# A fixed order for the first product of a one-core decoder trunk, with x in five loads

## Chip, core and metric

One of the eight cores of one Trainium2 chip runs the whole program, batch 1, 256 tokens, float32. The time is the device time of one execution in microseconds (us). The engines named below are PE (TensorE, the matrix engine, with PEld for its weight loads), DVE (VectorE), ACT (ScalarE), POOL (GpSimd) and SP (SyncE, which here only issues DMAs). "ACTq" and "SPq" are the instruction queues of those engines, on which DMA issues and waits stand in line with everything else.

## What is computed

One layer of a macaron block, then a final norm. All weights are float32, D_MODEL is 2048, D_FF is 5632:

```python
def swiglu(h, w_gate, w_up, w_down):
    return (jax.nn.silu(h @ w_gate) * (h @ w_up)) @ w_down

x = x + 0.5 * swiglu(rmsnorm(x, ffn1_norm), ffn1_w_gate, ffn1_w_up, ffn1_w_down)
x = x + hybrid_mixer(rmsnorm(x, mix_norm), w_in, conv_w, pool_w, pool_scale, w_out)
x = x + 0.5 * swiglu(rmsnorm(x, ffn2_norm), ffn2_w_gate, ffn2_w_up, ffn2_w_down)
return rmsnorm(x, final_norm)
```

The change touches the very first product, `x @ ffn1_w_gate` for the first 512 of its 5632 columns, and the way to it.

## The kernel before

**Tiles.** x lies in four tiles `xr[n]`, each 128 tokens x 2 x 512 channels. A product has the tokens as output rows, so the left operand is x transposed, 128 channels (one k of 16) by 256 tokens. The full float32 precision comes from three products per k: every operand is split into a high part that the matrix engine takes (`wh`, `xh`) and the remainder (`wl`, `xl`), and `gemm` (L142) adds hi x wh, lo x wh and hi x wl. With two blocks of 128 tokens that is 6 matmuls per k and 96 for one block of 512 columns (`ag` for the gate, `au` for up, `ad` for down).

**Weights.** `gemm` loads four k at a time into a tile `wt` (L174, on SP's queue, four buffers); ACT copies it to `wh` (L180) and DVE forms `wl` (L181). A `wt` buffer is free for the next load once `wl` is made.

**The first product.** Here the left operand does not exist yet. `first_block` loads x tile by tile, and `gained(..., at_once=True)` (L245) lets PE transpose a tile of 512 channels into one PSUM tile `tp` (8 transposes, L230), then per 128 channels ACT writes `xh` with the norm's gain as a scale (L252) and DVE writes `xl` (L253). The gains come from `prm`, which is itself a transposed load of `rows` (L80, `pp` L87, L88). The weights of this product are cut into 1, 1, 2, 4, 4 and 4 k. While nothing has arrived PE transposes an identity 14 times (`spin`, L101). ACT's queue also issues the DMA of `pw` (L334, used only in the mixer) and the four later parameter rows (L80).

**What sets the order.** A scheduler that simulates the program places the instructions of each engine, so those of different k, and of `ag` and `au`, stand interleaved. Both readers of `tp` carry waits: within one `tp` tile the `xh` of a block waits for the `xl` of the block before it. All else (`ffn` L276, `mixer` L329) runs on the same `gemm`.

Of the kernel before, what the change touches and what calls it, by code (L numbers as in the profile page):

```python
# [1 line left out]

# [6 lines left out]
F32 = mybir.dt.float32  # L9
F32R = mybir.dt.float32r  # L10
# [14 lines left out]
def hybrid_trunk(ctx, tc, x, ffn1_norm, ffn1_w_gate, ffn1_w_up, ffn1_w_down, mix_norm, w_in,  # L25
# [34 lines left out]
    def load_x(n):  # L60
        nc.sync.dma_start(out=xr[n], in_=xv[:, :, n * NB:(n + 1) * NB])


    small, col = [], {}
# [7 lines left out]
    NP = sum(r.shape[0] for r in small)  # L72
    prm = pool.tile([P, NP], F32, name="prm")

    def load_params(which, at):
        n = sum(r.shape[0] for r in which)
        rows = pool.tile([n, P], F32, name="rows", tag="rows", bufs=1)
        r0 = 0
        for v in which:
            nc.scalar.dma_start(out=rows[r0:r0 + v.shape[0], :], in_=v)  # L80
            r0 += v.shape[0]
        return rows, at, n

# [3 lines left out]
        nc.tensor.transpose(pp[:, :n], rows, ident[:n, :n])  # L87
        nc.vector.tensor_copy(out=prm[:, at:at + n], in_=pp[:, :n])  # L88

    first_params = load_params(small[:1], 0)  # L90
    load_x(0)
    ident = pool.tile([P, P], F32, name="ident")
    make_identity(nc, ident)
    mhalf = pool.tile([P, T], F32, name="mhalf")
# [4 lines left out]
    spin = tp_tile("spin")
    for i in range(14):  # L100
        nc.tensor.transpose(spin[:, :P], ident, ident)  # L101
    place_params(first_params)

# [34 lines left out]
    later = []  # L140

    def gemm(lhs, w, n0, ks, name, cuts=None, before=None, by_tile=None):  # L142
# [25 lines left out]
        cuts = cuts or [CH] * (nk // CH)  # L168
        for ci, m in enumerate(cuts):
            kk = ks[c0:c0 + m]  # L170
            if before:
                before(kk[0])
            wt = stat.tile([P, CH, NB], F32, name="wt", tag="wt", bufs=4)
            nc.sync.dma_start(  # L174
                out=wt[:, :m],
                in_=w[kk[0] * P:(kk[-1] + 1) * P, n0:n0 + NB].rearrange("(k p) n -> p k n", p=P))
            wh = stat.tile([P, CH, NB], F32R, name="wh", tag="wh", bufs=3)
            wl = stat.tile([P, CH, NB], F32R, name="wl", tag="wl", bufs=3)
            with nullcontext() if before else tc.high_priority():
                high[0] = nc.scalar.activation(out=wh[:, :m], in_=wt[:, :m], func=AF.Copy)  # L180
                nc.vector.tensor_sub(out=wl[:, :m], in0=wt[:, :m], in1=wh[:, :m].bitcast(F32))  # L181
            if by_tile and ci >= len(cuts) - 3:
                held.append((c0, kk, wh, wl))
            else:
                for i, k in enumerate(kk):
                    for t in range(T):
                        products(t, c0 + i, [k], wh[:, i:i + 1], wl[:, i:i + 1])
            c0 += m
            step()
        if by_tile:  # L190
            for t in range(T):
                for h in held:
                    products(t, *h)
                by_tile(t, acc_of[t])
        return acc
# [46 lines left out]
                                    in_=sv[a * Q:(a + 1) * Q, :, :, j, :])  # L242
        return dst

    def gained(n, c0, at_once=False):  # L245

        tp = transposed(xr[n]) if at_once else turned(xr[n], work([P, 4, S], "xt"))
        hi = stat.tile([P, 4, S], F32R, name="xh", tag="xh", bufs=4)
        lo = stat.tile([P, 4, S], F32R, name="xl", tag="xl", bufs=4)
        for i in range(4):  # L250
            g = prm[:, c0 + 4 * n + i:c0 + 4 * n + i + 1]
            nc.scalar.activation(out=hi[:, i, :], in_=tp[:, i, :], func=AF.Copy, scale=g)  # L252
            nc.vector.scalar_tensor_tensor(out=lo[:, i, :], in0=tp[:, i, :], scalar=g,  # L253
                                           in1=hi[:, i, :].bitcast(F32), op0=ALU.mult,
                                           op1=ALU.subtract)
        return hi, lo

# [4 lines left out]
    def block_of(tiles):  # L262
        def block(k):
            while k // 4 not in tiles:
                step()
            hi, lo = tiles[k // 4]
            return hi[:, k % 4, :], lo[:, k % 4, :]
        return block

    def residual(acc, n, factor, ts=range(T)):  # L270
# [2 lines left out]
                                           in1=xr[n][:, t, :], op0=ALU.mult, op1=ALU.add)  # L273


    def ffn(xt, rs, wg, wu, wd, after, cuts=None, before=None, last_tile=None):  # L276

        ht = {}  # L280

        def hidden(j, **first):
            ag = gemm(block_of(xt), wg, j * NB, range(KD), "ag", **first)
# [24 lines left out]
            later.append(turn)  # L308

        for j0 in range(0, FB, 6):  # L310
            js = range(j0, min(j0 + 6, FB))
            for j in js:
                hidden(j, **(dict(cuts=cuts, before=before) if j == 0 else {}))
            ks = range(4 * js[0], 4 * js[-1] + 4)
            done = js[-1] == FB - 1
            for n in range(DN):
                if done and n == DN - 1 and last_tile:
                    def tile_done(t, acc, n=n):
                        residual(acc, n, 0.5, [t])
                        last_tile(t)  # L320
                    gemm(block_of(ht), wd, n * NB, ks, "ad", by_tile=tile_done)
                    continue
                acc = gemm(block_of(ht), wd, n * NB, ks, "ad")
                residual(acc, n, 0.5)
                if done:
                    after(n)


    def mixer(l, xt, rs_of, after):  # L329
# [198 lines left out]
    def first_block(k):
        if k % 4 == 0:
            n = k // 4  # L530
            if n:
                load_x(n)
            xt[n] = gained(n, col["ffn1", 0], at_once=True)
# [88 lines left out]
```

## Time and profile before

| | us |
|---|---|
| median of 3 runs (1793.63 to 1793.72) | 1793.68 |
| the profiled execution | 1793.22 |
| its span, first to last instruction | 1791.1 |
| PE busy in it | 1776.9 (99%) |
| DVE busy | 1144.3 (64%) |
| ACT busy | 748.6 (42%) |

PE's busy share says that it nearly always has a matmul in flight, not that each is as fast as it can be; a row with 0.39 us duration stands 0.23 us after the row before it, since matmuls overlap. Only gaps on PE, and changes of its clock, can make this program longer or shorter.

### The profile page before, as it was taken

The page shows a single profiled execution, that of the slowest core. Times are in us where ns is not written, and L with a number is a line of the kernel's source. Part 1 is how long each engine was busy: PE and PEld are TensorE (multiplying, and loading weights), DVE is VectorE, ACT ScalarE, POOL GpSimd, SP SyncE. Part 2 cuts the span into 40 slices and gives each one's busy share as a digit, 9 for nine tenths or more (in the row PEclk, how much of TensorE's full clock was granted, in tenths as well). Part 3 has the DMA queues.
Part 4 walks back from the last instruction along what each step waited for, and adds up shares of the span by engine and source line. Part 5 has one row for each costly group of instructions (what it writes and reads, how often), then busy time and mean ns, then how long its engine had stood idle before and what let it go on. Part 6 is the DMA issues. An engine that isn't in the chain of part 4 may idle for free.

```text
span 1791.1 us, 19137 instructions
## 1 busy us (share of the span) xinstructions
PE 1776.9 (99%) x7928; PEld 1464.4 (82%) x7928; DVE 1144.3 (64%) x1260; ACT 748.6 (42%) x598; POOL 5.5 (0%) x19
## 2 busy tenths in 40 slices
PE   8999999999999999999999999999999999999998
PEld 7888888888888888887778888888888888888886
DVE  5766666444666687768767896666664446666653
ACT  6434433333344344545544455443443334433342
POOL 0000000000000000000000000000000000000000
PEclk9999999999999999999999999999999999999999
DMA  8655555555555555554545555555556555555652
GB/s 289 211 189 196 199 192 188 190 201 196 188 190 198 198 181 195 197 199 146 188 141 188 167 207 190 188 188 194 198 197 209 189 189 196 199 191 188 218 197 78
DMA packets 172262, 342.32 MB, mean 191 GB/s; under 512 B 5456, under 2 KB 6032, under 8 KB 172176
## 3 DMA queue, kind: packets, MB, share of 16 engines
q1 hardware_dynamic: 171232, 339.76, 56.2%
q10 hardware_dynamic: 944, 1.34, 0.3%
q8 instruction: 62, 1.02, 0.2%
q14 instruction: 24, 0.20, 0.0%
HBM read 338.98 MB, written 2.10 MB: 190 GB/s over the span
## 4 chain that ended last, share of the span: by engine, by line
PE 98%; DVE 1%; DMA 0%; ACT 0%; issue 0%; ACTq 0%; POOLq 0%
PE au L164 9%; PE ad L166 9%; PE au L165 9%; PE ad L164 9%; PE au L166 9%; PE ad L165 9%; PE ag L166 9%; PE ag L164 9%; PE ag L165 9%; PE az L164 4%; PE az L166 4%; PE az L165 4%; PE ao L166 1%; PE ao L165 1%; PE ao L164 1%; DVE wl L181 0%
## 5 line engine op out<-in xcount | busy, mean ns | idle before, releaser
L181 DVE TENSOR_TENSOR wl<-wt,wh 128x2048 fp32r<-128x2048 f32 (+1 forms) x322 | 732.8, 2277 | 543.4 <-ACT wh L180 541.4
L180 ACT ACTIVATE wh<-wt 128x2048 fp32r<-128x2048 f32 (+1 forms) x322 | 613.6, 1905 | 867.0 <-PE au L165 281.3
L164 PE MATMUL ag<-wh,xh 128*128 128x512 f32 x704 | 274.8, 390 | 2.1 <-ACT xh L252 2.1
L165 PE MATMUL ag<-wh,xl 128*128 128x512 f32 x704 | 274.6, 390 | 0.3 <-DVE xl L253 0.3
L166 PE MATMUL ag<-wl,xh 128*128 128x512 f32 x704 | 274.5, 390 | 0.2 <-DVE wl L181 0.2
L164 PE MATMUL au<-wh,xh 128*128 128x512 f32 x704 | 274.0, 389 | 0.0
L165 PE MATMUL au<-wh,xl 128*128 128x512 f32 x704 | 273.9, 389 | 0.0
L166 PE MATMUL au<-wl,xh 128*128 128x512 f32 x704 | 273.9, 389 | 0.0
L165 PE MATMUL ad<-wh,hl 128*128 128x512 f32 x704 | 273.9, 389 | 0.0
L164 PE MATMUL ad<-wh,hh 128*128 128x512 f32 x704 | 273.9, 389 | 0.0
L166 PE MATMUL ad<-wl,hh 128*128 128x512 f32 x704 | 273.7, 389 | 0.0
L241 DVE STREAM_TRANSPOSE ht<-h 32x256 f32<-32x256 f32 x352 | 153.5, 436 | 5.6
L164 PEld LDWEIGHTS ag<-wh,xh 128*128 128x128 f32 x704 | 132.4, 188 | 29.7 <-ACT xh L252 2.4
L166 PEld LDWEIGHTS ag<-wl,xh 128*128 128x128 f32 x704 | 132.5, 188 | 28.0 <-DVE wl L181 0.6
L165 PEld LDWEIGHTS ag<-wh,xl 128*128 128x128 f32 x704 | 132.4, 188 | 28.1 <-DVE xl L253 0.8
L165 PEld LDWEIGHTS ad<-wh,hl 128*128 128x128 f32 x704 | 132.2, 188 | 27.5
L164 PEld LDWEIGHTS au<-wh,xh 128*128 128x128 f32 x704 | 132.2, 188 | 27.5
L166 PEld LDWEIGHTS au<-wl,xh 128*128 128x128 f32 x704 | 132.2, 188 | 27.4
L166 PEld LDWEIGHTS ad<-wl,hh 128*128 128x128 f32 x704 | 132.2, 188 | 27.4
L165 PEld LDWEIGHTS au<-wh,xl 128*128 128x128 f32 x704 | 132.2, 188 | 27.3
L164 PEld LDWEIGHTS ad<-wh,hh 128*128 128x128 f32 x704 | 132.2, 188 | 27.3
L164 PE MATMUL az<-wh,xh 128*128 128x512 f32 x320 | 126.8, 396 | 0.0
(116 smaller groups left out, 1142.1 us busy)
## 6 DMA issues: line engine op xcount, KB each, us to landing
wt<-in_ffn_w_up_dram SPq DMA_DIRECT2D x88, 1024.0 KB, 5.1
wt<-in_ffn_w_down_dram SPq DMA_DIRECT2D x88, 1024.0 KB, 5.1
wt<-in_ffn_w_gate_dram SPq DMA_DIRECT2D x87, 1024.0 KB, 5.1
wt<-in_w_in_dram SPq DMA_DIRECT2D x40, 1024.0 KB, 5.0
wt<-in_w_out_dram SPq DMA_DIRECT2D x16, 1024.0 KB, 5.1
x<-in_x_dram SPq DMA_DIRECT2D x4, 512.0 KB, 10.3
out_dram<-xg SPq DMA_DIRECT2D x8, 256.0 KB, 3.1
gf<-in_final_norm_dram ACTq DMA_DIRECT2D x2, 512.0 KB, 4.7
```

What stands on the lines that cost most here:

```text
L164: nc.tensor.matmul(acc_of[t][:, t, :], lhsT=hi[:, ts], rhs=wh[:, i, :], start=first, stop=False)
L165: nc.tensor.matmul(acc_of[t][:, t, :], lhsT=lo[:, ts], rhs=wh[:, i, :], start=False, stop=False)
L166: nc.tensor.matmul(acc_of[t][:, t, :], lhsT=hi[:, ts], rhs=wl[:, i, :], start=False, stop=last)
L180: high[0] = nc.scalar.activation(out=wh[:, :m], in_=wt[:, :m], func=AF.Copy)
L181: nc.vector.tensor_sub(out=wl[:, :m], in0=wt[:, :m], in1=wh[:, :m].bitcast(F32))
L241: nc.vector.transpose(out=dv[j * Q:(j + 1) * Q, :, :, a, :], in_=sv[a * Q:(a + 1) * Q, :, :, j, :])
```

## The change

The first product gets a function of its own, `opening`, whose instructions stay in the order in which they are written (`manual_schedule`). x is loaded in five pieces: the first tile in two halves, then three whole tiles, between weight loads of 1, 1, 2, 2, 2, 2, 2, 2 and 2 k. Each 128 channels of `xh` and `xl` have a tile of their own. For a k the six matmuls run hi, hi, lo, lo, hi, hi over both token blocks. Of the identity transposes 12 stand ahead of the gains and 5 behind the first transposes of x. The later parameter rows go from ACT's queue to POOL's, and `pw` goes to SP's queue behind the last load of the first feed-forward. The second feed-forward no longer repeats eight sums of squares (`add_stats(ss0, n)`), which it did since a non-empty `first` was passed to it.

```diff
-    first_params = load_params(small[:1], 0)
-    load_x(0)
+    first_params = load_params(small[:1], 0, nc.scalar)
...
+    def opening(xt, c0, w, name):
+        acc = psum.tile([P, T, NB], F32, name=name, tag="acc", bufs=2)
+        pieces = {}
+        def prepare(n, blocks):
+            if n not in pieces:
+                pieces[n] = tp_tile("tp").rearrange("p (k s) -> p k s", k=4)
+                xt[n] = split_tiles()
+            for i in blocks:
+                for t in range(T):
+                    nc.tensor.transpose(pieces[n][:, i, t * P:(t + 1) * P],
+                                        xr[n][:, t, i * P:(i + 1) * P], ident)
+            return n, blocks
+        def ready(n, blocks):
+            gain_split(pieces[n], xt[n], n, c0, blocks)
+        def products(k, wh, wl, i):
+            hi, lo = (v[k % 4] for v in xt[k // 4])
+            for a, b, at in ((hi, wh, 0), (lo, wh, 1), (hi, wl, 2)):
+                for t in range(T):
+                    nc.tensor.matmul(acc[:, t, :], lhsT=a[:, t * P:(t + 1) * P], rhs=b[:, i, :],
+                                     start=k == 0 and at == 0, stop=k == KD - 1 and at == 2)
+        H = NB // 2
+        load_x(0, 0, H)
+        ws = {0: load_w(w, 0, [0])}
+        load_x(0, H, NB)
+        ws[1] = load_w(w, 0, [1])
+        ws[2] = load_w(w, 0, [2, 3])
+        load_x(1)
+        ws[4] = load_w(w, 0, [4, 5])
+        spin(12)
+        place_params(first_params)
+        prepare(0, [0, 1])
+        spin(5)
+        ready(0, [0])
+        h0 = split_w(ws[0], 1)
+        ready(0, [1])
+        h1 = split_w(ws[1], 1)
+        products(0, *h0, 0)
+        prepare(0, [2, 3])
+        ready(0, [2, 3])
+        h2 = split_w(ws[2], 2)
+        products(1, *h1, 0)
+        products(2, *h2, 0)
+        for k in range(3, KD):
+            if k % 4 == 3 and k + 1 < KD:
+                n = (k + 1) // 4
+                ws[k + 3] = load_w(w, 0, [k + 3, k + 4])
+                if n + 1 < DN:
+                    load_x(n + 1)
+                    ws[k + 5] = load_w(w, 0, [k + 5, k + 6])
+                prepare(n, range(4))
+                ready(n, range(4))
+            if k % 2:
+                products(k, *h2, 1)
+                if k + 1 < KD:
+                    h2 = split_w(ws[k + 1], 2)
+            else:
+                products(k, *h2, 0)
+        return acc
...
-            if first:
+            ag = first(wg) if first else gemm(block_of(xt), wg, j * NB, range(KD), "ag")
...
-        nc.scalar.dma_start(out=pw, in_=pool_w[l].rearrange("g c d -> c g d"))
+        with tc.issue_after(loaded[0].ins):
+            nc.sync.dma_start(out=pw, in_=pool_w[l].rearrange("g c d -> c g d"))
...
-        hi = stat.tile([P, 4, S], F32R, name="xh", tag="xh", bufs=4)
-        lo = stat.tile([P, 4, S], F32R, name="xl", tag="xl", bufs=4)
+        return ([stat.tile([P, S], F32R, name="xh", tag="xh", bufs=16) for i in range(4)],
+                [stat.tile([P, S], F32R, name="xl", tag="xl", bufs=16) for i in range(4)])
...
+    def begin(wg):
+        with tc.manual_schedule():
+            return opening(xt, col["ffn1", 0], wg, "ag")
...
-            more = load_params(small[1:], small[0].shape[0])
+            more = load_params(small[1:], small[0].shape[0], nc.gpsimd)
```

`load_w` and `split_w` are the load and the two split instructions of `gemm`; `gain_split` is the loop of `gained`.

ACT's queue from the first weights on, before. `waits` names the semaphores of an instruction: DMAHW a transfer, DVE, PE and Activation an engine. `tp_107` holds channels 0 to 511 of x, `tp_169` the next 512.

```order
L334 DMA pw_4654<-in_pool_w_dram 128x4x128
L180 ACTIVATE wh_128<-wt_126 128x512 [waits DMAHW2_49]
L80 DMA rows_460<-in_mix_norm_dram 16x128 [waits DMAHW1_49,DMAHW0_49,PE_49]
L80 DMA rows_460<-in_ffn2_norm_dram 16x128 [waits DMAHW3_49]
L252 ACTIVATE xh_116<-tp_107,prm_68 128x256 [waits DVE_49,PE_49]
L180 ACTIVATE wh_140<-wt_138 128x512 [waits DMAHW4_49]
L80 DMA rows_460<-in_conv_w_dram 12x128 [waits DMAHW5_49]
L180 ACTIVATE wh_152<-wt_150 128x1024
```

ACT's queue from the first weights (behind the first `xh`) to those of k = 4 to 7, in the change; `tp_117` is the first tile of x, `tp_183` the second.

```order
L153 ACTIVATE wh_138<-wt_91 128x512 [waits DMAHW2_49]
L329 ACTIVATE xh_119<-tp_117,prm_68 128x256 [waits DVE_49]
L153 ACTIVATE wh_144<-wt_94 128x512 [waits DMAHW4_49]
L329 ACTIVATE xh_120<-tp_117,prm_68 128x256 [waits DVE_49,PE_49]
L329 ACTIVATE xh_121<-tp_117,prm_68 128x256 [waits DVE_49]
L153 ACTIVATE wh_162<-wt_96 128x1024 [waits DMAHW5_49]
L329 ACTIVATE xh_184<-tp_183,prm_68 128x256 [waits PE_49]
L329 ACTIVATE xh_185<-tp_183,prm_68 128x256 [waits DVE_49]
L329 ACTIVATE xh_186<-tp_183,prm_68 128x256 [waits DVE_49]
L329 ACTIVATE xh_187<-tp_183,prm_68 128x256 [waits DVE_49]
L153 ACTIVATE wh_214<-wt_99 128x1024 [waits DMAHW7_49,Activation_49]
L153 ACTIVATE wh_230<-wt_178 128x1024 [waits DMAHW0_49,Activation_49]
```

The DMA issues are gone from ACT's queue, and the four `xh` of a tile stand together ahead of the next two weight copies; before, the `xh` of two tiles alternate there and a weight copy of four k stands among them:

```order
L252 ACTIVATE xh_178<-tp_169,prm_68 128x256 [waits PE_49]
L252 ACTIVATE xh_116<-tp_107,prm_68 128x256 [waits DVE_49]
L252 ACTIVATE xh_178<-tp_169,prm_68 128x256 [waits DVE_49]
L252 ACTIVATE xh_116<-tp_107,prm_68 128x256 [waits DVE_49]
L180 ACTIVATE wh_190<-wt_188 128x2048 [waits DMAHW7_49,Activation_49]
L252 ACTIVATE xh_178<-tp_169,prm_68 128x256 [waits DVE_49]
```

PE in the change, from the transposes of x's second tile to k = 4 (`wh_162` holds k = 2 and 3, `wh_214` k = 4 and 5).

```order
L168 MATMUL tp_183<-ident_71,x1_65 128x128 [waits DMAHW6_49]
L168 MATMUL tp_183<-ident_71,x1_65 128x128 x7
L179 MATMUL ag_89<-wh_162,xh_121 128x512 x2
L179 MATMUL ag_89<-wh_162,xl_125 128x512 x2
L179 MATMUL ag_89<-wl_163,xh_121 128x512 x2
L179 MATMUL ag_89<-wh_214,xh_184 128x512 [waits Activation_49]
L179 MATMUL ag_89<-wh_214,xh_184 128x512
L179 MATMUL ag_89<-wh_214,xl_188 128x512 [waits DVE_49]
L179 MATMUL ag_89<-wh_214,xl_188 128x512
L179 MATMUL ag_89<-wl_215,xh_184 128x512 [waits DVE_49]
L179 MATMUL ag_89<-wl_215,xh_184 128x512
```

Between the transposes of a tile and the first matmul that needs it stand the six matmuls of one k. Before, 18 matmuls of three k stood between the transposes of the second tile and those of the third, and after those of the third all 24 of the second tile:

```order
L230 MATMUL tp_219<-ident_72,x2_66 128x128 [waits DMAHW0_49,PE_49]
L230 MATMUL tp_219<-ident_72,x2_66 128x128 x7
L164 MATMUL ag_106<-wh_190,xh_178 128x512 [waits Activation_49]
L165 MATMUL ag_106<-wh_190,xl_179 128x512
L166 MATMUL ag_106<-wl_191,xh_178 128x512 [waits DVE_49]
```

So a tile's `xh`, `xl` had a whole tile's products ahead of them on PE before, and have one k's products now. From the first `au` on, but for the `ag` rows that stood among them, PE's rows read as before.

## Rows read from the trace of the kernel before

**Rows 1.** The page, its parts 1 and 4: engines, and the chain that ended last.
```profile
PE 1776.9 (99%) x7928; PEld 1464.4 (82%) x7928; DVE 1144.3 (64%) x1260; ACT 748.6 (42%) x598; POOL 5.5 (0%) x19
...
PE 98%; DVE 1%; DMA 0%; ACT 0%; issue 0%; ACTq 0%; POOLq 0%
```

**Rows 2.** Waits of PE: what waited for what, us in total, times, longest.
```profile
PE ag L164 <- ACT xh L252: 2.1, 1, 2.1
...
PE tp L230 <- DMA x<-in_x_dram: 0.8, 1, 0.8
PE ao L166 <- DVE wl L181: 0.6, 1, 0.6
...
PE ag L166 <- DVE wl L181: 0.2, 1, 0.2
```

**Rows 3.** The chain in order of time: start us, us, what.
```profile
1.29 6.60 DMA pw<-in_pool_w_dram
...
7.91 0.33 ACTq L80
...
8.87 0.80 PE ag L164
...
24.27 0.87 PE tp L230 x8
```

**Rows 4.** The timeline of PE: start us, us, what, count, [idle before].
```profile
4.65 0.28 PE L87 MATMUL pp<-ident,rows 16*128 16x16 f32 x1
...
5.69 1.06 PE L230 MATMUL tp<-ident,x 128*128 128x128 f32 x8 [0.76 <-DMA x<-in_x_dram]
...
15.94 0.39 PE L164 MATMUL ag<-wh,xh 128*128 128x512 f32 x1
16.17 0.39 PE L165 MATMUL ag<-wh,xl 128*128 128x512 f32 x1
...
35.87 0.39 PE L164 MATMUL au<-wh,xh 128*128 128x512 f32 x1
```

**Rows 5.** Busy time by engine in short stretches, then PEclk, DMA share, GB/s.
```profile
3.00:4.00 1.00, 1.00 (x7) 1.00 (x6) 0.00 (x0) 0.00 (x0) 0.00 (x0) 1.00 0.84 247
...
8.00:9.00 1.00, 0.13 (x1) 0.13 (x1) 0.15 (x1) 0.66 (x2) 0.00 (x0) 0.71 1.06 410
9.00:10.00 1.00, 1.00 (x3) 0.67 (x4) 0.96 (x2) 0.34 (x1) 0.00 (x0) 0.50 1.06 404
...
11.00:12.00 1.00, 1.00 (x6) 0.66 (x5) 0.36 (x1) 0.97 (x2) 0.00 (x0) 0.58 1.04 380
```

**Rows 6.** The timeline of ACT, columns as in Rows 4.
```profile
6.52 0.63 ACT L180 ACTIVATE wh<-wt 128x512 fp32r<-128x512 f32 x1 [3.79 <-DMA wt<-in_ffn_w_gate_dram]
...
10.55 1.06 ACT L180 ACTIVATE wh<-wt 128x1024 fp32r<-128x1024 f32 x1 [1.22 <-DMA wt<-in_ffn_w_gate_dram]
...
18.38 0.47 ACT L252 ACTIVATE xh<-tp,prm 128x256 fp32r<-128x256 f32 x1 [1.42 <-PE tp L230]
19.36 0.87 ACT L252 ACTIVATE xh<-tp,prm 128x256 fp32r<-128x256 f32 x2 [0.51 <-DVE xl L253]
```

**Rows 7.** The timeline of DVE, columns as in Rows 4.
```profile
7.18 0.69 DVE L181 TENSOR_TENSOR wl<-wt,wh 128x512 fp32r<-128x512 f32 x1 [2.04 <-ACT wh L180]
8.85 0.48 DVE L253 SCALAR_TENSOR_TENSOR xl<-tp,prm,xh 128x256 fp32r<-128x256 f32 x1 [0.98 <-ACT xh L252]
...
11.64 1.22 DVE L181 TENSOR_TENSOR wl<-wt,wh 128x1024 fp32r<-128x1024 f32 x1 [1.58 <-ACT wh L180]
```

**Rows 8.** PE's instructions on `ag`, then on `au`, up to 36 us: busy, count, clock.
```profile
0.00:36.00 36.00, 21.13 (x79) 0.95 0.94 330
...
0.00:36.00 36.00, 3.82 (x16) 0.95 0.94 330
```

**Rows 9.** Eight squares at the start of the second feed-forward, and PE there.
```profile
L212 ACT ACTIVATE junk<-x x8: 611/631/632, 1071.2 to 1080.6; 128x512 bf16<-128x512 f32 x8
...
1060.00:1080.00 20.00, 20.00 (x90) 16.58 (x89) 17.96 (x29) 13.29 (x25) 0.85 (x1) 1.00 0.57 194
```

More of the change, by code (lines that the diff above doesn't have):

```diff
@@ L1 @@
-from contextlib import ExitStack, nullcontext
+from contextlib import ExitStack
 import concourse.bass as bass
@@ L58, in hybrid_trunk, with load_x @@
     xv = x[0].rearrange("(t p) d -> p t d", p=P)
-    def load_x(n):
-        nc.sync.dma_start(out=xr[n], in_=xv[:, :, n * NB:(n + 1) * NB])
+    def load_x(n, c0=0, c1=NB):
+        nc.sync.dma_start(out=xr[n][:, :, c0:c1], in_=xv[:, :, n * NB + c0:n * NB + c1])
     small, col = [], {}
@@ L73, in hybrid_trunk, with load_params @@
     prm = pool.tile([P, NP], F32, name="prm")
-    def load_params(which, at):
+    def load_params(which, at, queue):
         n = sum(r.shape[0] for r in which)
@@ L79, in load_params @@
         for v in which:
-            nc.scalar.dma_start(out=rows[r0:r0 + v.shape[0], :], in_=v)
+            queue.dma_start(out=rows[r0:r0 + v.shape[0], :], in_=v)
             r0 += v.shape[0]
@@ L98, in hybrid_trunk, with spin @@
     nc.scalar.activation(out=early, in_=mhalf, func=AF.Silu)
[L99 to L102, printed above, removed]
+    def spin(n):
+        dst = psum.tile([P, T, NB], F32, name="spin", tag="acc", bufs=2)
+        for i in range(n):
+            nc.tensor.transpose(dst[:, 0, :P], ident, ident)
     NK = 3 * P
@@ L139, in hybrid_trunk, with load_w, split_w @@
     high = [None]
+    loaded = [None]
     later = []
-    def gemm(lhs, w, n0, ks, name, cuts=None, before=None, by_tile=None):
+    def load_w(w, n0, kk):
+        wt = stat.tile([P, CH, NB], F32, name="wt", tag="wt", bufs=4)
+        loaded[0] = nc.sync.dma_start(
+            out=wt[:, :len(kk)],
+            in_=w[kk[0] * P:(kk[-1] + 1) * P, n0:n0 + NB].rearrange("(k p) n -> p k n", p=P))
+        return wt
+    def split_w(wt, m):
+        wh = stat.tile([P, CH, NB], F32R, name="wh", tag="wh", bufs=3)
+        wl = stat.tile([P, CH, NB], F32R, name="wl", tag="wl", bufs=3)
+        high[0] = nc.scalar.activation(out=wh[:, :m], in_=wt[:, :m], func=AF.Copy)
+        nc.vector.tensor_sub(out=wl[:, :m], in0=wt[:, :m], in1=wh[:, :m].bitcast(F32))
+        return wh, wl
@@ L147, in bank_pair, with gemm @@
+    def gemm(lhs, w, n0, ks, name, by_tile=None):
         def bank_pair():
@@ L166, in products @@
                 nc.tensor.matmul(acc_of[t][:, t, :], lhsT=hi[:, ts], rhs=wl[:, i, :], start=False, stop=last)
-        cuts = cuts or [CH] * (nk // CH)
+        cuts = [CH] * (nk // CH)
         for ci, m in enumerate(cuts):
             kk = ks[c0:c0 + m]
[L171 to L181, printed above, removed]
+            wt = load_w(w, n0, kk)
+            with tc.high_priority():
+                wh, wl = split_w(wt, m)
             if by_tile and ci >= len(cuts) - 3:
@@ L243, in turned, with split_tiles, gained, gain_split @@
         return dst
-    def gained(n, c0, at_once=False):
-        tp = transposed(xr[n]) if at_once else turned(xr[n], work([P, 4, S], "xt"))
-        hi = stat.tile([P, 4, S], F32R, name="xh", tag="xh", bufs=4)
-        lo = stat.tile([P, 4, S], F32R, name="xl", tag="xl", bufs=4)
-        for i in range(4):
+    def split_tiles():
+        return ([stat.tile([P, S], F32R, name="xh", tag="xh", bufs=16) for i in range(4)],
+                [stat.tile([P, S], F32R, name="xl", tag="xl", bufs=16) for i in range(4)])
+    def gained(n, c0):
+        return gain_split(turned(xr[n], work([P, 4, S], "xt")), split_tiles(), n, c0)
+    def gain_split(tp, tiles, n, c0, blocks=range(4)):
+        hi, lo = tiles
+        for i in blocks:
             g = prm[:, c0 + 4 * n + i:c0 + 4 * n + i + 1]
-            nc.scalar.activation(out=hi[:, i, :], in_=tp[:, i, :], func=AF.Copy, scale=g)
-            nc.vector.scalar_tensor_tensor(out=lo[:, i, :], in0=tp[:, i, :], scalar=g,
-                                           in1=hi[:, i, :].bitcast(F32), op0=ALU.mult,
+            nc.scalar.activation(out=hi[i], in_=tp[:, i, :], func=AF.Copy, scale=g)
+            nc.vector.scalar_tensor_tensor(out=lo[i], in0=tp[:, i, :], scalar=g,
+                                           in1=hi[i].bitcast(F32), op0=ALU.mult,
                                            op1=ALU.subtract)
@@ L266, in block @@
             hi, lo = tiles[k // 4]
-            return hi[:, k % 4, :], lo[:, k % 4, :]
+            return tuple(v[k % 4] if isinstance(v, list) else v[:, k % 4, :] for v in (hi, lo))
         return block
@@ L273, in residual, with ffn, hidden @@
                                            in1=xr[n][:, t, :], op0=ALU.mult, op1=ALU.add)
-    def ffn(xt, rs, wg, wu, wd, after, cuts=None, before=None, last_tile=None):
+    def ffn(xt, rs, wg, wu, wd, after, begin=None, last_tile=None):
         ht = {}
-        def hidden(j, **first):
-            ag = gemm(block_of(xt), wg, j * NB, range(KD), "ag", **first)
+        def hidden(j, first=None):
+            ag = first(wg) if first else gemm(block_of(xt), wg, j * NB, range(KD), "ag")
             if first:
@@ L312, in ffn @@
             for j in js:
-                hidden(j, **(dict(cuts=cuts, before=before) if j == 0 else {}))
+                hidden(j, begin if j == 0 else None)
             ks = range(4 * js[0], 4 * js[-1] + 4)
@@ L526, in hybrid_trunk @@
     ss0, xt, r0 = new_stats(), {}, []
[L528 to L533, printed above, removed]
+    def begin(wg):
+        with tc.manual_schedule():
+            return opening(xt, col["ffn1", 0], wg, "ag")
     def first_rs():
@@ L582, in hybrid_trunk @@
     for l in range(DEPTH):
-        start = dict(cuts=[1, 1, 2, 4, 4, 4], before=first_block) if l == 0 else {}
         x1, r1 = phase("mix", l, lambda a: ffn(xt, rs, ffn1_w_gate[l], ffn1_w_up[l], ffn1_w_down[l],
-                                               a, **start))
+                                               a, begin if l == 0 else None))
         x2, r2 = phase("ffn2", l, lambda a: mixer(l, x1, r1, a))
```

## The prediction

> **What bounds the kernel now.** I read the page first: PE is busy 99% of the span and 98% of the chain that ended last [rows 1]. So only a gap on PE, or a lower clock, costs or gives time. The waits of PE say where the gaps are: all but one of its six lie in the first 20 us, the longest 2.1 us for the first `xh`, and the one outside (0.6 us, in the output product of the mixer) has nothing to do with the change [rows 2]. The chain in order of time shows what stood before that `xh`: the transfer of `pw`, from 1.29 to 7.89 us, then a parameter DMA issue on ACT's queue at 7.91, and the first product only at 8.87 [rows 3]. The order rows say why: that issue waits for a transfer and stands ahead of the first `xh`, which itself needs only transposes that were done at 6.75 (5.69 + 1.06) [rows 4]. Last, PE's clock: granted 1.00 up to some point after 8 us, 0.50 in the microsecond from 9, back in the one from 11 [rows 5]. [...]
>
> **A mark to measure by.** PE's rows from the first `au` on are the same in both programs, so the whole question is when PE has 96 matmuls of the opening behind it. At 36.0 us 79 + 16 = 95 have begun [rows 8], the last at 35.87 [rows 4]; one stands 0.23 us after another (16.17 - 15.94) [rows 4], so number 97 starts at 36.3. The sum below finds the same start in the change. In a dense stretch a tile of x with 24 matmuls and 8 transposes (0.87 us [rows 3]) would take 24 x 0.2275 + 0.87 = 6.33 us.
>
> **The head, up to the transposes of x's second tile.** `pw` and the four parameter issues leave ACT's queue. The first half of x's first tile is 256 KB. Before, 512 KB had arrived at 5.69 [rows 4], while the queues moved some 250 GB/s [rows 5]; half as much could be there about a microsecond earlier. The gains cannot be earlier than `pp` at 4.65 [rows 4]. So the first transposes start between 4.8 and 5.7; I take 5.0. From there, with the durations of [rows 6, 7] and 0.03 us from engine to engine (what 19.36 - 18.38 leaves after 0.47 and 0.48):
> four transposes to 5.57; `xh` 0 to 6.1; `wh` of k = 0 (0.63) to 6.6, and `xl` 0 (0.48) to 6.6; `xh` 1 waits for `xl` 0, to 7.1; `wh` of k = 1 to 7.65; on DVE `wl` 0 (0.69) to 7.35, `xl` 1 to 7.75, `wl` 1 to 8.4. PE starts k = 0 at 6.65, not 8.87, six matmuls to 8.0, four transposes to 8.45, k = 1 to 9.8. Then it waits: `xh` 2 starts at 8.6, `xh` 3 after `xl` 2, to 10.15; only then ACT copies `wh` of k = 2 and 3 (1.06), to 11.1. PE has k = 2 behind it after `wl` (1.22, to 12.35) at 12.85. Call this T0: 18 matmuls and one tile of transposes are done. Before, the 19th matmul started at 15.94 [rows 4] with one more tile transposed, so 15.94 - 0.87 = 15.07 compares. The head gains 2.2 us. Bounds: transposes at 4.8 or 5.7 (-0.2, +0.7), the weights of k = 0 as late as before at 6.52 instead of 6.0 (+0.5), those of k = 2 and 3 at 10.55 instead of 10.1 (+0.45) [rows 6].
>
> **The three tiles behind it.** This is where I expect the loss. Before, the scheduler let the `xh` of two tiles alternate and had a whole tile of products for PE meanwhile. Now PE transposes a tile, does one k, and needs the next weights, whose `wh` stands on ACT behind the four `xh` of the tile just transposed. And these four do not follow each other freely: each waits on DVE for the `xl` of the block before. The trace has one such pair: an `xh` at 18.38, its successor at 19.36, after an idle 0.51 put down to `xl` [rows 6]. So one step is 0.98 us, not 0.47. Counted from T0: transposes 0.87, six matmuls 1.37, PE is out of work at 2.24. The first `xh` starts when all eight transposes have ended (1.06), at 1.07; the fourth ends at 1.07 + 3 x 0.98 + 0.47 = 4.48; `wh` of two k (1.06, overlapping by 0.1) at 5.44; PE goes on at 5.49. That is 3.25 us of idle PE. Four matmuls last to 6.40, `wl` (1.22 behind `wh`) ends at 6.70, PE waits 0.34 more, and 14 matmuls later, at 9.93, the next tile begins. The next `wh`, `wl` (6.5 and 7.9) are in time. So 9.93 instead of 6.33 us, 3.6 lost per tile, three times: 10.8 us. Bounds 9.8 and 10.3, by 0 to 0.06 us per hand-over.
>
> **The rest.** `au` starts at T0 + 3 x 9.93 + 1.37 (k = 15) = 44.0; against 36.3 that is +7.7. The two views agree: -2.2 and +10.8, less about 0.9 for the waits after 16 us and the later `pp` that before paid on PE and that now fall into idle time. Costed at nothing: the transfers (the weights of k = 4 and 5 are needed at 17.2, and 2.5 MB at the 380 GB/s of [rows 5] have long passed), the parameter issues on POOL (needed by `pp` at the end of `ag`), `pw` among the mixer's weights, and the eight squares that the second feed-forward loses: PE is dense there, 20.00 of 20 us [rows 9], so nobody waited for them. Single tiles for `xh`, `xl` free their buffers no later. If the cover of PE's work after 44 us were gone, `wl` of the first `au` weights would have to come after 44; at twice the rows of two k it ends near T0 + 2 x 9.93 + 10.7 = 43.4, which is close, and worth some tenths at most.
>
> **The clock.** Three times PE now stands still for 3.25 us, longer than the 2.1 us after which the clock stood at 0.50 before. The six matmuls from 8.87 [rows 3], at 0.43 apart, took 2.8 us to 11.69 in place of 1.37: 1.45 us. In a tile 0.3 of it hides in the wait for `wl`, and the stretch can be a little longer (0.50 and 0.71, 0.58 around it [rows 5]): 1.3 us each. Before the standstill there was only light work then, transposes; here there are 20 matmuls, so I don't count every one: two of three, +2.6. Bounds 0 and 3 x 1.45.
> [...]
>
> **Sum.** 7.7 + 2.6 = +10.3. On the profiled execution (1793.22) that is 1803.5; the median lies 0.46 higher, so 1804.0 for the median.
>
> **Rivals.**
> First, the earlier start wins: the `xh`, `xl` of a tile hide behind the products as they do now, PE waits nowhere in the three tiles, and only the head's gain and the 0.9 us remain: -3.1, 1790.6 us, faster than before. It decides at one point: whether PE is idle between k = 3 and k = 4. For it speaks that all transfers are early; against it the order rows, where `wh` stands behind four `xh` and PE behind `wh`. 5%.
> Second, ACT keeps its order, but the waits for `xl` cost nothing (the pair from 19.36, which comes from two tiles, takes 0.87, so a step is 0.40): the fourth ends at 2.74, PE idles 1.5 and 0.35 us per tile, T0 is 12.2, and `au` starts at 12.2 + 3 x 8.18 + 1.37 = 38.1: +1.8, 1795.5, no change to be told. Against it stands the idle 0.51 in [rows 6]. 7%.
> Third, the clock falls in every tile, for 1.45 us: +12.0, 1805.7. 22%.
> Fourth, it never falls: +7.7, 1801.4. 20%.
>
> **How the numbers follow.** The forecast (one or two falls) has 43%, the rivals 54%, and 3% is left for slower outcomes that I don't see. With the bounds of head, hand-overs and clock: 7.7 - 0.2 - 0.4 = +7.1 (1800.8) to 7.7 + 1.65 + 1.1 + 4.35 = +14.8 (1808.5). Range 1800.5 to 1808.5. A measurement of this kernel tells 0.2%, 3.6 us, from no change: faster than 1790.1 2%, between 11%, slower than 1797.3 87%.
>
> **What would show it.** Right: PE's first `ag` matmul near 6.6; three waits of about 3 us of `ag` for ACT `wh` in PE's waits; on ACT a tile's `xh` about 1 us apart with idle time put down to `xl`; the first `au` near 44 or later; granted clock below 1 in some microseconds between 15 and 45. The head is wrong if the first product starts after 7.5, the tiles if `xh` follow each other in 0.4 us, the rest if PE has new waits after 50 us. A PE without gaps from 13 us on would make the whole prediction wrong.

## The result, and the profile after

The changed kernel takes **1806.41 us** (median of 6 runs, 1804.64 to 1807.18), the kernel before beside it 1793.7 (6 runs, 1793.07 to 1793.88): a ratio of 1.007, 95% interval 1.0061 to 1.008. It is 12.7 us slower; the prediction was 10.3 and 1804.0, with a range of 1800.5 to 1808.5. The execution profiled after took 1806.23, its span is 1804.4. One execution in this document, 6412.11 us of the kernel with single tiles below, stands far outside all others and is left out of every range; nothing on record says why.

The page, its parts 1 and 4, as in [rows 1], says almost nothing of it. PE stays at 99% of the span; its 5.5 us more of busy time are mostly matmuls that took longer.

```profile
PE 1782.4 (99%) x7931; PEld 1467.3 (81%) x7931; DVE 1145.3 (63%) x1263; ACT 744.4 (41%) x585; POOL 7.7 (0%) x23
...
PE 97%; DVE 1%; ACT 1%; DMA 0%; issue 0%; SPq 0%; ACTq 0%; POOLq 0%
```

The waits of PE, as in [rows 2] (us in total, times, longest), do: the list now starts with the wait that the prediction named, `ag` for `wh`, and has no new one behind the opening.

```profile
PE ag L179 <- ACT wh L153: 11.0, 5, 3.2
...
PE ao L245 <- DVE wl L154: 0.6, 1, 0.6
```

PE's timeline, to be read beside [rows 4] (start us, us, what, count, [idle before]):

```profile
4.34 0.83 PE L168 MATMUL tp<-ident,x 128*128 128x128 f32 x4
...
6.25 0.73 PE L179 MATMUL ag<-wh,xh 128*128 128x512 f32 x2 [0.54 <-ACT wh L153]
...
10.90 0.73 PE L179 MATMUL ag<-wh,xh 128*128 128x512 f32 x2 [0.92 <-ACT wh L153]
...
12.73 1.04 PE L168 MATMUL tp<-ident,x 128*128 128x128 f32 x8
...
18.35 1.21 PE L179 MATMUL ag<-wh,xh 128*128 128x512 f32 x2 [3.20 <-ACT wh L153]
19.36 1.05 PE L179 MATMUL ag<-wh,xl 128*128 128x512 f32 x2
20.21 1.05 PE L179 MATMUL ag<-wl,xh 128*128 128x512 f32 x2
...
24.18 1.03 PE L168 MATMUL tp<-ident,x 128*128 128x128 f32 x8
...
29.80 1.22 PE L179 MATMUL ag<-wh,xh 128*128 128x512 f32 x2 [3.21 <-ACT wh L153]
...
36.66 1.03 PE L168 MATMUL tp<-ident,x 128*128 128x128 f32 x8
...
42.44 1.22 PE L179 MATMUL ag<-wh,xh 128*128 128x512 f32 x2 [3.17 <-ACT wh L153]
...
49.54 0.39 PE L243 MATMUL au<-wh,xh 128*128 128x512 f32 x1
```

The reader is to see four things. The first product starts 2.6 us earlier than before (6.25, was 8.87). Three tiles of x begin at 12.73, 24.18 and 36.66, each followed by a standstill of 3.2 us. Behind a standstill two matmuls stand 0.85 us after the two before them (20.21 - 19.36), not 0.46. And the first `au`, the mark of the prediction, starts at 49.54, not at 36.3. What lies behind the mark is unchanged to 0.1 us: 1804.4 - 49.54 = 1754.9 us now, 1791.1 - 36.3 = 1754.8 before.

Why PE stands still is on ACT's timeline, to be read beside the pair at 18.38 and 19.36 in [rows 6]. The four `xh` of a tile follow each other 1.02 to 1.03 us apart, 0.55 of it idle and put down to `xl`, and only behind the fourth comes the `wh` that PE waits for:

```profile
13.80 0.47 ACT L329 ACTIVATE xh<-tp,prm 128x256 fp32r<-128x256 f32 x1 [2.96 <-PE tp L168]
14.83 0.47 ACT L329 ACTIVATE xh<-tp,prm 128x256 fp32r<-128x256 f32 x1 [0.55 <-DVE xl L330]
15.86 0.47 ACT L329 ACTIVATE xh<-tp,prm 128x256 fp32r<-128x256 f32 x1 [0.55 <-DVE xl L330]
16.88 0.47 ACT L329 ACTIVATE xh<-tp,prm 128x256 fp32r<-128x256 f32 x1 [0.55 <-DVE xl L330]
17.25 1.99 ACT L153 ACTIVATE wh<-wt 128x1024 fp32r<-128x1024 f32 x2
```

Last the clock, in one-microsecond windows as in [rows 5] (the value after POOL's is PEclk). It stood at 0.50 behind each of the three standstills, and behind the second for six whole microseconds:

```profile
18.00:19.00 1.00, 0.65 (x2) 0.56 (x3) 0.67 (x1) 1.00 (x2) 0.00 (x0) 0.70 0.00 0
19.00:20.00 1.00, 1.00 (x4) 0.80 (x3) 1.00 (x2) 0.25 (x1) 0.00 (x0) 0.50 0.00 0
...
21.00:22.00 1.00, 1.00 (x4) 0.78 (x3) 0.00 (x0) 0.00 (x0) 0.00 (x0) 0.59 0.96 307
...
29.00:30.00 1.00, 0.20 (x1) 0.21 (x2) 0.54 (x2) 1.00 (x2) 0.00 (x0) 0.50 0.00 0
...
34.00:35.00 1.00, 1.00 (x4) 0.80 (x3) 0.00 (x0) 0.00 (x0) 0.00 (x0) 0.50 1.05 410
35.00:36.00 1.00, 1.00 (x5) 0.74 (x4) 0.00 (x0) 0.00 (x0) 0.00 (x0) 0.77 0.98 354
...
43.00:44.00 1.00, 1.00 (x4) 0.77 (x3) 1.00 (x2) 1.00 (x2) 0.00 (x0) 0.50 0.00 0
...
45.00:46.00 1.00, 1.00 (x4) 0.76 (x4) 0.84 (x1) 0.97 (x4) 0.00 (x0) 0.65 0.79 195
```

### The profile page after: what moved, and what is told of

It reads as the page before. It is cut to its first block, busy times and chain, and to the rows that moved or that the text cites. A ratio compares the mean times of both kernels' runs of the same rounds, so it can differ in the third digit from the quotient of the medians.

```text
span 1804.4 us, 19150 instructions
## 1 busy us (share of the span) xinstructions
PE 1782.4 (99%) x7931; PEld 1467.3 (81%) x7931; DVE 1145.3 (63%) x1263; ACT 744.4 (41%) x585; POOL 7.7 (0%) x23
## 3 DMA queue, kind: packets, MB, share of 16 engines
q8 instruction: 62, 1.02, 0.2%
## 4 chain that ended last, share of the span: by engine, by line
PE 97%; DVE 1%; ACT 1%; DMA 0%; issue 0%; SPq 0%; ACTq 0%; POOLq 0%
PE ad L245 9%; PE au L243 9%; PE au L244 9%; PE ad L244 9%; PE au L245 9%; PE ad L243 9%; PE ag L243 8%; PE ag L244 8%; PE ag L245 8%; PE az L243 4%; PE az L245 4%; PE az L244 4%; PE ao L245 1%; PE ao L244 1%; PE ao L243 1%; PE ag L179 1%
## 5 line engine op out<-in xcount | busy, mean ns | idle before, releaser
L154 DVE TENSOR_TENSOR wl<-wt,wh 128x2048 fp32r<-128x2048 f32 (+2 forms) x325 | 733.2, 2258 | 538.5 <-ACT wh L153 536.5
L153 ACT ACTIVATE wh<-wt 128x2048 fp32r<-128x2048 f32 (+2 forms) x325 | 613.7, 1889 | 861.7 <-PE au L244 279.8
L243 PE MATMUL ag<-wh,xh 128*128 128x512 f32 x672 | 261.4, 389 | 0.0
L244 PE MATMUL ag<-wh,xl 128*128 128x512 f32 x672 | 261.4, 389 | 0.0
L245 PE MATMUL ag<-wl,xh 128*128 128x512 f32 x672 | 261.4, 389 | 0.0
L245 PEld LDWEIGHTS ag<-wl,xh 128*128 128x128 f32 x672 | 126.1, 188 | 26.3
L243 PEld LDWEIGHTS ag<-wh,xh 128*128 128x128 f32 x672 | 126.1, 188 | 26.2
L244 PEld LDWEIGHTS ag<-wh,xl 128*128 128x128 f32 x672 | 126.1, 188 | 26.1
```

## The experiments

The theory had three parts: PE waits because `wh` stands behind four `xh`; the `xh` are slow because each waits for an `xl`; the standstill brings the clock down. Each was taken away alone, then the useful edits were joined, and the parts that the prediction had costed at nothing were put into the kernel before.

**Order on ACT and DVE.** In the changed kernel the weights of the next two k are split ahead of the tile's `xh`, `xl`; everything else stays.

```diff
                 prepare(n, range(4))
+                ahead = split_w(ws[k + 1], 2)
                 ready(n, range(4))
             if k % 2:
                 products(k, *h2, 1)
-                if k + 1 < KD:
+                if k % 4 == 3:
+                    h2 = ahead
+                elif k + 1 < KD:
                     h2 = split_w(ws[k + 1], 2)
```

> The changed kernel with one move: in each of the three later tiles of x, ACT and DVE split the weights of the next two k ahead of the tile's four xh and xl, not behind them. Theory (PE stands still because wh stands behind four serial xh on ACT, and the clock falls after that): the three waits of 3.2 us become about 0.6 us before the second pair of k (its wh still stands behind the xh) and 0.35 us for wl, the clock stays at 1.00, and 13 to 14 us go: 1792 to 1793.5 us. Rival (it is the fixed order itself, without au products to fill in, or the smaller weight loads): the three waits stay near 3 us and the time within 3 us of 1806.

Measured: 1794.24 us (10 runs, 1793.72 to 1794.52), before 1793.66; ratio 1.0004, interval 0.9994 to 1.0013. One line's place takes 12.2 of the 12.7 us away. Its waits of PE, and PE with its clock from 5 to 45 us (busy, PEclk, DMA share, GB/s):

```profile
PE ag L179 <- ACT wh L153: 2.3, 4, 1.1
...
PE au L248 <- DVE wl L154: 0.3, 1, 0.3
```
```profile
5.00:45.00 40.00, 37.01 (x167) 1.00 0.85 298
```

The rival, the fixed order itself or the smaller weight loads, is out: both are still there, and the waits of 3.2 us are gone. The time lies 0.7 us above the theory's range. Of the four waits for `wh`, three are those in the tiles, foreseen at 0.6 and now 0.2 to 0.5; the fourth, 1.1, stands in the head, where the changed kernel has 0.92. Not foreseen was a wait of the first `au` products for `wl`, and behind the mark (36.88 here) this execution takes 1792.3 - 36.88 = 1755.4 us, half a microsecond more than the two above; its tiles also begin 0.3 us later, at 12.99. The clock's 1.00 is borne out by the rows: in the tiles a pair of matmuls stands 0.46 us after the pair before it.

**One PSUM tile or two.** The order of the changed kernel stays, but the transposes of a tile go into two `tp` tiles, and ACT and DVE take the blocks 0, 2, 1, 3, so that an `xh` and the `xl` before it read different PSUM tiles.

```diff
-                pieces[n] = tp_tile("tp").rearrange("p (k s) -> p k s", k=4)
+                pieces[n] = [tp_tile("tp").rearrange("p (k s) -> p k s", k=4) for _ in range(2)]
...
-            gain_split(pieces[n], xt[n], n, c0, blocks)
+            for i in ([0, 2, 1, 3] if len(blocks) == 4 else blocks):
+                gain_split(pieces[n][i // 2], xt[n], n, c0, [i])
```

> The changed kernel with the transposes of a tile of x in two PSUM tiles (two blocks of 128 channels in each), and its xh and xl made in the order 0, 2, 1, 3, so that an xh no longer stands behind the xl just before it; the order of xh and wh on ACT is unchanged. Theory: the step from one xh to the next goes from 1.02 us to about 0.45, the waits of PE from 3.2 to about 1.3 us, and the idle time falls by 2 us in each of three tiles; with standstills that short the clock stays up: 1794 to 1796. If the clock still falls each time: 1799 to 1801. Rival (the serial readers of PSUM cost nothing, ACT's order alone does): the waits stay above 2.5 us and the time above 1803.

Measured: 1795.44 us (10 runs, 1795.17 to 1797.41), ratio 1.0011, interval 1.0001 to 1.002: as the theory expected, and the rival is out. ACT's four `xh` of a tile now take 1.94 us together, where they took 16.88 + 0.47 - 13.80 = 3.55; PE's standstill falls from 3.20 to 1.14 (1.16 in the second tile), and the clock stays at 1.00, with pairs of matmuls 0.46 us apart behind the standstill:

```profile
13.60 1.94 ACT L330 ACTIVATE xh<-tp,prm 128x256 fp32r<-128x256 f32 x4 [2.52 <-PE tp L168]
15.44 1.99 ACT L153 ACTIVATE wh<-wt 128x1024 fp32r<-128x1024 f32 x2
```
```profile
16.54 0.73 PE L180 MATMUL ag<-wh,xh 128*128 128x512 f32 x2 [1.14 <-ACT wh L153]
```
```profile
5.00:45.00 40.00, 34.84 (x161) 1.00 0.80 280
```

So the step of 1.02 us is the wait of one reader of a PSUM tile for the other, and without it the changed kernel is 11 us faster in its own order, the clock that then stays up among them. The wait goes by the tile and not by what is read: each `xh` reads other columns of `tp` than the `xl` that it waited for, with 0.55 us of idle time each. With two `tp` tiles no idle time stands among the four (1.94 us for the row of x4); in the head of the same run, where the third and the fourth `xh` still share a tile, ACT idles 0.55 us for the `xl` before the fourth, which starts at 9.67.

**The clock by itself.** In the changed kernel twelve more matmuls, into a PSUM tile that nothing reads, follow k = 3, 7 and 11. They keep PE at work while it would wait, and end before `wh` is there.

```diff
+        def fill(m, hi, wh):
+            dst = psum.tile([P, T, NB], F32, name="fill", tag="acc", bufs=2)
+            for i in range(m):
+                nc.tensor.matmul(dst[:, 0, :], lhsT=hi[:, :P], rhs=wh[:, 1, :], start=True, stop=True)
...
+                if k % 4 == 3 and k + 1 < KD:
+                    fill(12, xt[k // 4][0][3], h2[0])
```

> The changed kernel with 12 more matmuls of 512 columns, on operands at hand and into an unused PSUM tile, behind the products of k = 3, 7 and 11, where PE stands still. They delay nothing, since 12 x 0.23 = 2.7 us is less than the wait. Theory (the clock falls because PE stands still, and costs some 5.5 us): granted clock 1.00 from 5 us on, waits of 0.6 us where 3.2 stood, time 1800.5 to 1801.5. Rival (the clock falls for another reason, or its fall is hidden): 1806 as before, or later by what the added matmuls delay.

Measured: 1801.65 us (4 runs, 1801.61 to 1801.67), ratio 1.0045, interval 1.003 to 1.006: 0.15 above the range that the theory expected, with the tiles beginning 0.27 us later than in the changed kernel (13.00, was 12.73). PE in the three tiles, and the clock from 5 to 45 us:

```profile
13.00 1.04 PE L168 MATMUL tp<-ident,x 128*128 128x128 f32 x8
...
15.25 2.88 PE L185 MATMUL fill<-wh,xh 128*128 128x512 f32 x12
18.63 0.73 PE L179 MATMUL ag<-wh,xh 128*128 128x512 f32 x2 [0.50 <-ACT wh L153]
...
23.20 1.04 PE L168 MATMUL tp<-ident,x 128*128 128x128 f32 x8
...
28.83 0.73 PE L179 MATMUL ag<-wh,xh 128*128 128x512 f32 x2 [0.47 <-ACT wh L153]
...
33.44 1.03 PE L168 MATMUL tp<-ident,x 128*128 128x128 f32 x8
...
39.07 0.73 PE L179 MATMUL ag<-wh,xh 128*128 128x512 f32 x2 [0.31 <-ACT wh L153]
...
45.00 0.39 PE L250 MATMUL au<-wh,xh 128*128 128x512 f32 x1
```
```profile
5.00:45.00 40.00, 36.84 (x169) 1.00 0.63 220
```

The products of k = 4 start 5.63 us behind the tile's transposes (18.63 - 13.00), as in the changed kernel (18.35 - 12.73 = 5.62): the extra matmuls took no time of their own, and the wait for `wh` is the same. Only the fall of the clock is gone. By the medians it costs 1806.41 - 1801.65 = 4.8 us. Tile by tile, from the first matmul behind the wait to the next tile, and to `au` for the third: 24.18 - 18.35 = 5.83 against 23.20 - 18.63 = 4.57; then 36.66 - 29.80 = 6.86 against 33.44 - 28.83 = 4.61; then 49.54 - 42.44 = 7.10 against 45.00 - 39.07 = 5.93. That is 1.26, 2.25 and 1.17, together 4.7.

**A better order.** In the changed kernel the weights of k + 1 are split ahead of the tile's `xh`, `xl`, those of k + 3 between its second and its third block.

```diff
-                ready(n, range(4))
-            if k % 2:
-                products(k, *h2, 1)
-                if k + 1 < KD:
-                    h2 = split_w(ws[k + 1], 2)
-            else:
-                products(k, *h2, 0)
+                pair = [split_w(ws[k + 1], 2)]
+                ready(n, [0, 1])
+                pair.append(split_w(ws[k + 3], 2))
+                ready(n, [2, 3])
+            products(k, *h2, k % 2)
+            if k % 2 and k + 1 < KD:
+                h2 = pair.pop(0)
```

> The changed kernel with the weights of the next two k split ahead of a later tile's four xh and xl, and those of the two k after that split between its second and third. Theory (order on ACT decides): against e1_weights_first the waits before the second pair of k (0.5 us and 0.3 for wl, three times) go too, PE has no gap over 0.5 us between 13 and 30 us, clock 1.00: 1792 to 1792.8, below the kernel before by 1 to 1.5 us. Rival (what is left against the kernel before is the head or the smaller loads): as e1, 1794 or more.

Measured: 1792.09 us (11 runs, 1791.6 to 1792.26), before 1793.56; ratio 0.9992, interval 0.9984 to 1.0001. That is as the theory expected; the interval just includes no change, but all eleven runs lie below all 29 of the kernel before (1793.0 to 1794.0). The tiles on PE are now 6.37 us apart, and 6.33 was the prediction's figure for a dense one:

```profile
12.70 1.03 PE L168 MATMUL tp<-ident,x 128*128 128x128 f32 x8
...
19.07 1.04 PE L168 MATMUL tp<-ident,x 128*128 128x128 f32 x8
...
25.44 1.04 PE L168 MATMUL tp<-ident,x 128*128 128x128 f32 x8
```

**The same in the head.** As the last, and the weights of k = 2 and 3 split ahead of the first tile's fourth block.

```diff
-        ready(0, [2, 3])
+        ready(0, [2])
         h2 = split_w(ws[2], 2)
+        ready(0, [3])
```

> As e5_interleaved, and the weights of k = 2 and 3 split between the third and the fourth xh of the first tile. The wait of PE before k = 2 (1.15 us in e1_weights_first) falls to about 0.2 us: 1 us less than e5, 1791 to 1791.8. If the transposes of the second tile or a transfer are last then, the time equals e5's.

Measured: **1791.65 us** (11 runs, 1791.36 to 1792.02), ratio 0.999, interval 0.9982 to 0.9999. The time lies in the expected range, but the gain over the last kernel is 0.4 us and not the 1 us that was expected. PE's wait before k = 2 is gone and the second tile's transposes start at 12.35, not 12.70, but that tile then takes 6.61 us, not 6.37 (the next begins at 18.96). It is the fastest kernel of the study: some 1.9 us ahead of the kernel before (1793.56 beside it), with an interval that just excludes no change.

**The queues alone.** In the kernel before, the later parameters go to POOL's queue and `pw` to SP's.

```diff
-            nc.scalar.dma_start(out=rows[r0:r0 + v.shape[0], :], in_=v)
+            queue.dma_start(out=rows[r0:r0 + v.shape[0], :], in_=v)
...
-        nc.scalar.dma_start(out=pw, in_=pool_w[l].rearrange("g c d -> c g d"))
+        with tc.issue_after(loaded[0].ins):
+            nc.sync.dma_start(out=pw, in_=pool_w[l].rearrange("g c d -> c g d"))
```

> The kernel before with one part of the change: the later parameter rows issue on POOL's queue and the pool weights on SP's behind the first feed-forward, so no DMA issue but the first stands on ACT's queue. Theory (the first product waited for a parameter issue on ACT that waited for the pool weights): first product near 7.2 us in place of 8.87, and the gain reaches the end: 1791.5 to 1792.5. Rival (the first weights or the next tile of x would then be the last to arrive): 1793 to 1794, with a new wait of PE between 7 and 15 us.

Measured: 1793.03 us (10 runs, 1792.34 to 1793.55), ratio 0.9996, interval 0.9987 to 1.0006: less than expected, within the rival's range, and by the interval not told from no change. The rival's new wait of PE is not in the trace, though. On ACT the scheduler put both first `wh` ahead of the first `xh`, so PE starts at 7.97, 0.9 us earlier than before, and the clock falls here too, with a standstill of 1.22 us; the last tile's transposes start 0.6 us earlier than before, at 23.52, where the timeline of the kernel before has 24.11. ACT's rows, PE's, and PE's windows from 8 us on:

```profile
6.29 1.27 ACT L181 ACTIVATE wh<-wt 128x512 fp32r<-128x512 f32 x2 [3.57 <-DMA wt<-in_ffn_w_gate_dram]
7.46 0.46 ACT L253 ACTIVATE xh<-tp,prm 128x256 fp32r<-128x256 f32 x1
```
```profile
7.97 0.49 PE L165 MATMUL ag<-wh,xh 128*128 128x512 f32 x1 [1.22 <-ACT xh L253]
...
23.52 1.03 PE L231 MATMUL tp<-ident,x 128*128 128x128 f32 x8
```
```profile
8.00:9.00 1.00, 0.73 (x2) 0.69 1.05 408
9.00:10.00 1.00, 1.00 (x3) 0.50 1.07 399
```

**What was costed at nothing.** The kernel before with a tile of its own for each `xh`, `xl`, and without the eight repeated squares (left out: nothing reads their sums a second time).

```diff
-        hi = stat.tile([P, 4, S], F32R, name="xh", tag="xh", bufs=4)
-        lo = stat.tile([P, 4, S], F32R, name="xl", tag="xl", bufs=4)
+        hi = [stat.tile([P, S], F32R, name="xh", tag="xh", bufs=16) for i in range(4)]
+        lo = [stat.tile([P, S], F32R, name="xl", tag="xl", bufs=16) for i in range(4)]
...
-                hidden(j, **(dict(cuts=cuts, before=before) if j == 0 else {}))
+                hidden(j, **(dict(cuts=cuts, before=before) if j == 0 and cuts else {}))
```

> The kernel before with two parts of the change alone: single tiles for each 128 channels of xh and xl, and no repeated sums of squares at the start of the second feed-forward. Both were costed at nothing: 1793.2 to 1794.0. Rival (the repeated squares, or buffers that free sooner, hide gaps that PE's busy time does not show): outside that by more than 1 us.

Measured: 1794.97 us (11 runs, 1794.75 to 1795.17), ratio 1.0008, interval 0.9999 to 1.0017. That is 1.4 us above the kernel before beside it (1793.56): the interval just includes no change, but all eleven runs lie above all 29 of that kernel (1793.0 to 1794.0). The second half of the edit was then run by itself:

```diff
-                hidden(j, **(dict(cuts=cuts, before=before) if j == 0 else {}))
+                hidden(j, **(dict(cuts=cuts, before=before) if j == 0 and cuts else {}))
```

> The kernel before without the eight repeated squares of the second feed-forward, which ACT alone computes in the middle of a stretch where PE is dense; PE's order is that of before, row for row. If they were covered (theory) the time is that of before, 1793.4 to 1793.9, and the +1.4 us of the run with single tiles belong to the tiles. If the squares have a part in that +1.4, this one is at 1794.5 or above.

Measured: 1793.41 us (10 runs, 1792.83 to 1793.55), before 1793.73, ratio 0.9998, interval 0.9989 to 1.0008. The squares were covered. So the rise belongs to the single tiles, and the trace of the kernel with them shows where: the scheduler places the opening in another order, and an `xh` of a later tile on ACT, and later a matmul of PE, now wait 2.39 and 1.27 us for an `xl` (before, the longest such waits were 0.51 and 0.29), and each time that `xl` stands on DVE behind a `wl` of four k. The rows of ACT, of DVE for the second of them, and of PE:

```profile
19.49 0.47 ACT L252 ACTIVATE xh<-tp,prm 128x256 fp32r<-128x256 f32 x1 [2.39 <-DVE xl L253]
```
```profile
21.80 2.29 DVE L181 TENSOR_TENSOR wl<-wt,wh 128x2048 fp32r<-128x2048 f32 x1 [1.32 <-ACT wh L180]
```
```profile
24.55 0.50 PE L165 MATMUL ag<-wh,xl 128*128 128x512 f32 x1 [1.27 <-DVE xl L253]
```

That the tiles cost this by the other order is read from these rows; a run with single tiles and the old order was not made.

## Why the prediction held, and where it did not

| step | predicted | measured |
|---|---|---|
| first product | 6.65 | 6.25 |
| T0, second tile's transposes | 12.85 | 12.73 |
| PE idle in each tile | 3.25 | 3.20, 3.21, 3.17 |
| `xh` to `xh` | 0.98 | 1.02 |
| a tile at full clock | 9.93 | 10.20, 10.24 (filled) |
| clock | 2 x 1.3 = 2.6 | 1.26 + 2.25 + 1.17 = 4.7 |
| first `au` | 44.0 + 2.6 = 46.6 | 49.54 |

**Bound.** Right. Reading PE's gaps and clock alone was enough; what lies behind the mark moved by 0.1 us.

**Head.** T0 was right to 0.12 us, in part by luck, since the steps to it were others; and 0.12 is within what executions differ by: in four other traces with the same head T0 is 12.70, 12.97, 12.99 and 13.00. The gains were there at 4.12, and the first transposes at 4.34, outside the bound of 4.8; but ACT then idled 0.93 us for the second weights, whose copy starts at 7.64, not 7.0, and that took the lead back. The prediction names one cause of the late start before, the parameter issue on ACT's queue. It is not the whole: with the queues alone moved in the kernel before, the first product stands at 7.97 and the time falls by 0.6 us, which the interval does not tell from none. The first transposes of x are at 5.68 there, at 4.34 in the change with its half tile.

**Tiles.** The mechanism was right in both its parts: taking away the order on ACT brings the time back to 1794.24, taking away the wait for `xl` to 1795.44. The idle time was foreseen to 0.1 us. The 0.3 us per tile that are missing lie in the `xh` step (1.02, not 0.98, three times) and in hand-overs, within the bound of 10.3. With T0 at 12.73, three tiles of 10.2 and k = 15, `au` would start at 44.7 at full clock; the clock's 4.7 make 49.4, and 49.54 was measured.

**The clock: the term that was mis-sized.** "I don't count every one: two of three" was the wrong choice. The row at hand showed a fall behind the one long standstill (0.50 behind 2.1 us), and the reason to expect fewer, that matmuls and not transposes come before it here, was an estimate that no row showed. For 3.2 us that did not help; whether it matters for shorter waits is not shown (see the last section). The clock fell three times in three, and one of these falls lasted nearly twice as long as that of before (until 5.7 us behind the first matmul; before, by the mean of 0.58 from 11 to 12, until 3.0), which the bound of 1.45 each had not foreseen; the sum of 4.7 lies above the 3 x 1.45 of the bounds. The third rival, at 1805.7, is therefore nearer to the 1806.41 than the forecast is. Behind the waits of 3.2 us the clock stood at 0.50 three times of three; behind the waits of 1.14 and 1.16 us, with two PSUM tiles, it stayed at 1.00, with pairs of matmuls 0.46 us apart.

**The first two rivals.** "The earlier start wins" was wrong for this order, and right for another: with the weight splits between the blocks the same opening takes 1791.65, where that rival had 1790.6. "The waits for `xl` cost nothing" had 1795.5, and the run without them 1795.44. The price of a tile was right (8.18 us there, 21.12 - 12.97 = 8.15 in that run), the condition was not met; that the totals agree to 0.1 us is luck, since its first `au` was 38.1 and stands at 38.78 in that run.

**The rest.** `pw`, the parameter issues on POOL and the squares show no wait of PE that was not there before, as said, and the squares alone made no change. Not counted was that the later gains' copy on DVE (39.31, 0.21 us) holds up an `xl` of the third tile: k = 12 starts 42.44 - 36.66 = 5.78 us behind the transposes, in the other tiles 5.62. That single tiles cost nothing under the fixed order is not shown, since no run of the changed kernel is without them; under the scheduler the kernel with them rose by 1.4 us.

## What to carry to other kernels

Where an order is written by hand, follow each operand of the next product back through its engine's queue: a 1-us copy that is needed first and stands behind four steps that wait for another engine costs all of them (here PE stood still for 3.2 us each time). A busy share of 99% hides a loss of 0.7%, so read the gaps and the clock in windows of the stretch that was changed. If PE must wait, count a fall of the clock for every standstill as long as one that brought it down in the trace at hand (2.1 us in that of before; all three of 3.2 us then brought one), or fill the wait. Read the clock from the distance between rows as well as from its record.

## What was not expected of the hardware

The granted clock does not come back after the same time. After standstills of 3.20, 3.21 and 3.17 us, and the same matmuls behind them, it stood at 0.50 until some 3.5, 5.7 and 3.3 us behind the first matmul (the windows from 21, 35 and 45 have means of 0.59, 0.77 and 0.65); why the second was longer stays open. In the second tile it had also fallen earlier: within the standstill (28.00 to 29.00 has a mean of 0.82), where in the others it fell in the microsecond in which PE went on (0.70 and 0.65). Falls of differing length may also be what spreads the changed kernel's six runs over 2.5 us: the mean granted clock on record is 0.994 in the two slowest and 0.995 in the other four, and the four runs with PE kept at work lie within 0.06. No profile of the other five shows it.

Shorter waits of nearly one length had different ends. 1.22 us behind transposes of x were followed by 0.50, in the run with the queues moved; three waits of 1.14 to 1.16 us behind matmuls, in the run with two PSUM tiles, were not. The two cases differ in the work before the wait, but also by 0.06 us in length and in their place: in the former PE had come to its full speed only a moment before (identity transposes at 0.24 us each up to 4.6, those of x at 0.13 from 5.68). Which of these decides is not shown.

And a granted clock of 1.00 has to be borne out by the rows. In the traces of the change and of the kernel before it reads 1.00 from the start, though the identity transposes there take twice the time of the later transposes of x (in the kernel before 14 in 3.25 us, and 8 in 0.87 from the first to the next product), and the same ones run faster later (in the change 12 in 2.82 us at first, 5 in 0.71 from 5.01). In the run of the kernel before without the repeated squares even the first product is so slow: 0.43 us from matmul to matmul, as at 0.50, in a window that reads 1.00.

```profile
10.12 0.63 PE L164 MATMUL ag<-wh,xh 128*128 128x512 f32 x1
10.55 0.63 PE L165 MATMUL ag<-wh,xl 128*128 128x512 f32 x1
```
```profile
10.00:11.00 1.00, 1.00 (x4) 1.00 1.05 387
```

So PE begins these executions at the lower speed, and when it leaves it differs: in the five traces with the head of the change as written, the first four transposes of x take 0.66 and 0.83 us in two, where the first product stands at 6.2, and 1.10 to 1.12 in three, where it stands at 6.5.
